# The MLP's operands at another place modulo 512 bytes, a third buffer for the block sums, and four sums in three operations

## The chip, the cores and the metric

The kernel runs on one core of a Trainium2 chip. The metric is the device time of one execution in microseconds (us); of the kernel before, three runs were timed, and the median counts. One more execution was recorded by the hardware profiler; all rows of a trace in this document come from such a recording. Engines are named as in the profile: PE is the matrix engine (PEld its weight loads), DVE the vector engine, ACT the scalar engine, POOL the GpSimd engine, SP the engine that issues most DMAs.

## The reference, cut to what matters

A two-layer encoder on 256 tokens of width 2048, in float32. Each layer has an attention block (neighbourhood attention in layer 0, grouped-query attention in layer 1, both beside four cross-attention heads into 256 memory tokens), an output projection, and a dense MLP of inner width 8192 with a squared ReLU:

```python
h = h + jnp.concatenate([mix, cross], axis=-1) @ w_o[i]
n = rms_norm(h, mlp_norm[i])
h = h + jnp.square(jax.nn.relu(n @ w_up[i])) @ w_down[i]
```

The change touches only what runs in and around the MLP.

## The kernel before, in words

**Precision.** Every float32 product is made of three matmuls in a reduced float32 format: each operand is split into a high and a low half (ACT copies the high half, L302; DVE subtracts it, L303), and high x high, high x low and low x high are added in PSUM. So each weight that comes in by DMA passes ACT and DVE once before PE reads it.

**Two shapes of matmul.** Each matmul has a stationary operand of 128x128, which a weight load (LDWEIGHTS) brings into PE, and a moving operand that streams through. In the first shape the weights stand still and 256 columns of activations move: the MLP's up-projection (L736 to L738, `ps_u<-hT,uh`: hT moves, uh and ul stand still) and the q, k and memory-key projections (L222 to L224, `ps_s`). In the second the activations stand still and 512 columns of weights move: the MLP's down-projection (L852 to L854, `p<-th,a_s`: th moves, a_s stands still), the value and output projections and the last eighth of the down-projection (L210 to L214, `ps_m`).

**The MLP.** The inner width is cut in 8 parts of 8 blocks of 128. `up_grains` computes one block with 48 matmuls (two grains of 24). `squared` applies ReLU and square on ACT, and for each pair of blocks forms four sums of their quarter blocks (L802, tile `c`) and splits seven of the eight quarters into `a_s`. The down-projection of the first seven parts uses a scheme with seven products in place of eight for each pair of blocks (p1 to p7): `down_grains` takes three blocks of weights as they are (tile `b`, split into bh and bl; 9 matmuls, products p3, p1 and p2) and four block sums (tile `t`, split into th and tl; 12 matmuls, products p5, p7, p6 and p4). Of the four sums one is the loaded fourth block plus another, added in the DMA itself (L832, issued on POOL), and three are formed on DVE (L831, L840, L841). At the end of each half part `taken` adds the seven PSUM banks into `h` or into the collectors z (DVE L875, L886, ACT), and `folded` combines the collectors at the very end. The eighth part is done with plain products (`plain_grains`).

**A step.** Outside the first part, the program alternates: 48 up matmuls of one block, then 12 with th and tl, then 9 with bh and bl. There are 56 such steps in a layer, 112 in all. They read, as the built program's allocation has it, at these addresses modulo 512 bytes: hT at 160, uh and ul at 480 and 224 (two buffers), and th, tl, bh, bl and a_s all at 128. (In the attention of layer 0, nT moves at 128 and hi and lo stand at 192 and 448.)

**Order and buffers.** A list of grains with fixed look-ahead (`SOON`) decides when loads, sums and splits are recorded; a scheduler then places the recorded instructions on their engines by its own timeline. Each engine runs its list in order. The tiles of the MLP lie in two pools: `mlp` (z, c, a_s or a_p, bh, bl, th, tl) and `side` (raw weights raw_U, b, t, and the splits uh, ul). The tag `T` in `side` holds t, the scaled rows h_s ahead of the MLP, and half of the plain weights (raw_T); it has two buffers of 8 KB per partition. Loads of t, b and raw_U share the queue of SP, which issues in order and holds there until a buffer is free.

**Names for offsets.** `half_of_side(raw, hf, place)` puts a split at `place` bytes into its buffer. MOVING_AT = 160 puts uh at 128 or 384 modulo 512 where it is the moving operand (plain products, and the first chunks of layer 1's projection); STILL_AT = 64 puts the ring's hi and lo at 192 or 448 where they stand still.

Of the kernel before, what the change touches and what calls it, by code (L numbers as in the profile page):

```python
# [17 lines left out]
P = 128  # L18
# [21 lines left out]
GUARD = 3  # L40

MOVING_AT = 160

STILL_AT = 64
MASKED = -1e30
# [29 lines left out]
def encoder_kernel(ctx: ExitStack, tc: tile.TileContext, t: dict, out: bass.AP):  # L75
# [4 lines left out]
    def opened(name, side="left", space=None, bufs=1):  # L80
        kw = {"space": space} if space else {}
        manager = tc.tile_pool(name=name, bufs=bufs, side=side, reuse_waits="tile", **kw)
        pools[name] = manager, manager.__enter__()
        return pools[name][1]
# [557 lines left out]
    def o_done(layer, nb):  # L642
        which = 2 * layer

        def guard():

            box["near"] = mean_square(which, GUARD, "near")
            box["scale"] = keep.tile([P, NT], F32, tag="scale", name="scale")
            nc.gpsimd.tensor_tensor(box["scale"], box["near"], mhalf[:, :NT], op=ALU.pow)
            box["hT"] = wide(f"hT{layer}")  # L650

        def begun():

            y = at.side.tile([P, NT, 512], F32, tag="T", bufs=2, name="h_s")
            for i in range(NT):
                nc.scalar.activation(y[:, i, :], h[:, i, D - 512 :], AF.Copy, scale=box["scale"][:, i : i + 1])
            box["begun"] = y

        def scaled(b):
            y = at.side.tile([P, NT, 512], F32, tag="T", bufs=2, name="h_s")  # L660
            for i in range(NT):
                nc.scalar.activation(y[:, i, :], h[:, i, b * 512 : (b + 1) * 512], AF.Copy,
                                     scale=box["scale"][:, i : i + 1])
            transposed(box["hT"], lambda i, k: y[:, i, k % 4 * P : (k % 4 + 1) * P],
                       list(range(b * 4, b * 4 + 4)), (G_M0, G_M1)[layer])

        def inv():

            v = mean_square(which, 4, "full")
            box["inv"] = keep.tile([P, NT], F32, tag="inv", name="inv")  # L670
            nc.vector.reciprocal(v, v)
            nc.vector.tensor_tensor(box["inv"], v, box["near"], op=ALU.mult)
            box["ninv"] = keep.tile([P, NT], F32, tag="ninv", name="ninv")
            nc.vector.tensor_scalar(box["ninv"], box["inv"], -1.0, None, op0=ALU.mult)

        def f(w):
            if nb == 0:
                closed("work")
                at.side = opened("side", side="right")
            def add():  # L680
                for i in range(NT):
                    hs = h[:, i, nb * 512 : (nb + 1) * 512]
                    nc.vector.tensor_tensor(hs, w.ps[i], hs, op=ALU.add)

            def squares():
                for i in range(NT):
                    sum_squares(which, i, nb)

            if nb < 3:
                add()  # L690
                squares()
            if nb == GUARD - 1:
                later(1, guard)
                for b in range(GUARD):
                    later(2 + 2 * b, scaled, b)
                later(7, begun)
            if nb == 3:
                y = box["begun"]
                for i in range(NT):
                    nc.vector.scalar_tensor_tensor(y[:, i, :], w.ps[i], box["scale"][:, i : i + 1], y[:, i, :],  # L700
                                                   op0=ALU.mult, op1=ALU.add)
                box["ready"] = transposed(box["hT"], lambda i, k: y[:, i, k % 4 * P : (k % 4 + 1) * P],
                                          list(range(12, KT)), (G_M0, G_M1)[layer])
                later(4, past, add)
                later(6, past, squares)
                later(8, past, inv)
        return f
# [36 lines left out]
        return tiles  # L744

    def loaded(src, tag):
        raw = at.side.tile([P, CH], F32, tag=tag, bufs=2, name=f"raw_{tag}")
        nc.sync.dma_start(raw, src)
        return raw

    def up_grains(layer, part, m):
        own = {}

        def load():
            own["raw"] = loaded(t[f"w_up{layer}"][part * PK + m], "U")

        def prep(hf):
            own[hf] = half_of_side(own["raw"], hf)

        def run(hf):  # L760
            if hf == 0:
                if part == 0:
                    own["ps"] = at.acc.tile([P, 512], F32, tag="acc", name="ps_u")[:, :SEQ]
                else:
                    if part == 1 and m == 0:
                        closed("ps_att", "ps_acc")
                        at.sums = opened("ps_sums", space=bass.MemoryType.PSUM)
                        box["ps"] = {}
                    own["ps"] = at.sums.tile([P, 512], F32, tag="up", name="ps_u")[:, :SEQ]
                    if part == 1 and m == 0:  # L770
                        box["first"] = {n: at.sums.tile([P, 512], F32, tag=n, name=n) for n in BANKS}
            u_products(own["ps"], hf * (KT // 2), KT // 2, *own.pop(hf))

        def after():
            if part == 0 and m == 0:
                closed("cat", "ring")
                at.mlp = opened("mlp")
                box["z"] = [at.mlp.tile([P, 4, 512], F32, tag=f"z{q}", name=f"z{q}") for q in range(2)]
                box["z_set"] = set()
            squared(layer, part, m, own["ps"])  # L780

        return [Grain(lambda: run(0), None, load, None, lambda: prep(0), SOON),
                Grain(lambda: run(1), after, None, None, lambda: prep(1), SOON)]

    def squared(layer, part, m, ps):

        e = m % 2
        if e == 0:
            box["c"] = at.mlp.tile([P, 8, P], F32, tag="c", bufs=2, name="c")
        c = box["c"]  # L790
        two = c[:, 2 * e : 2 * e + 2, :].rearrange("p a b -> p (a b)")
        nc.scalar.activation(two, ps, AF.Relu)
        nc.scalar.activation(two, two, AF.Square)
        if e == 0:
            return
        if part == PARTS - 1:
            a = at.mlp.tile([P, 2, 4, P], F32R, tag="a", bufs=6, name="a_p")
            split(a[:, 0], a[:, 1], c[:, :4])
        else:
            for d, x, y, op in ((4, 2, 0, ALU.subtract), (5, 1, 0, ALU.add), (6, 5, 2, ALU.subtract),  # L800
                                (7, 3, 6, ALU.subtract)):
                nc.vector.tensor_tensor(c[:, d, :], c[:, x, :], c[:, y, :], op=op)  # L802
            a = at.mlp.tile([P, 2, 7, P], F32R, tag="a", bufs=6, name="a_s")
            split(a[:, 0], a[:, 1], c[:, 1:])
        box["a", part, m // 2] = a
        if part == PARTS - 1 and m == PK - 1 and layer == 1:
            later(2, load_gf)

    def down_grains(layer, part, n, begins, ends):
# [4 lines left out]
        def load():  # L814
            src = t[f"w_pair{layer}"][(part * 2 + q) * STEPS + j]
            own["b"] = at.side.tile([P, 3 * 512], F32, tag="b", bufs=2, name="b")
            nc.sync.dma_start(own["b"], src[:, : 3 * 512])
            own["t"] = at.side.tile([P, 4, 512], F32, tag="T", bufs=2, name="t")
            nc.sync.dma_start(own["t"][:, 0, :], src[:, 3 * 512 :])

        def behind(fn):
# [71 lines left out]
    def folded(q):  # L893

        z1, z5, z6, z7 = (box["z"][q][:, n, :] for n in range(4))
        inv, ninv = box["inv"], box["ninv"]
        add_scaled(columns_of(1, q, 0), z1, inv[:, 1:2])
        nc.vector.tensor_tensor(z6, z6, z1, op=ALU.subtract)
        nc.vector.tensor_tensor(z7, z6, z7, op=ALU.subtract)
        nc.vector.tensor_tensor(z6, z6, z5, op=ALU.add)  # L900
        add_scaled(columns_of(1, q, 1), z6, inv[:, 1:2])
        add_scaled(columns_of(0, q, 0), z7, inv[:, 0:1])
        nc.vector.tensor_tensor(z7, z7, z5, op=ALU.add)
        add_scaled(columns_of(0, q, 1), z7, ninv[:, 0:1])

    def plain_grains(layer, nb):
# [8 lines left out]

        def prep(c, hf):
            if c == 0:
                own[c, hf] = half_of_side(own[0], hf, MOVING_AT)
            else:
                own[c, hf] = tuple(at.mlp.tile([P, HALF], F32R, tag="bt"[hf] + x, name=f"{x}_p") for x in "hl")  # L920
                split(*own[c, hf], own[1][:, hf * HALF : (hf + 1) * HALF])
# [351 lines left out]
```

## Time and profile before

| what | value |
|---|---|
| median of 3 runs | 2046.73 us (2046.35 to 2048.07) |
| the profiled execution | 2049.4 us, span 2047.6 us |
| PE busy | 2025.4 us, 99% of the span, 13044 matmuls |
| DVE busy | 1665.1 us, 81% |
| ACT busy | 1241.3 us, 61% |
| chain that ended last | PE 94%, DVE 3%, DMA 1% |

The span runs from the first to the last instruction of the core. A matmul's own duration in the trace holds its latency (0.28 us for 256 columns, 0.39 us for 512), and matmuls overlap; how fast they follow each other is read from their starts. In the answers of the timeline a row has start, duration, engine, line, operation, tiles and count. In a list of waits a row has who waited, for whom, the sum in us, the number of times and the longest. The groups of instructions have busy time and mean duration in ns, then the idle time of the engine ahead of them and who ended it.

### The profile page before, as it was taken

What the parts mean: (1) busy time and instruction counts of PE and PEld (TensorE: products, weight loads), DVE (VectorE), ACT (ScalarE), POOL (GpSimd) and SP (SyncE); (2) the same over time, 40 slices, a digit from 0 to 9 for tenths busy, and PEclk for the clock granted to TensorE, in tenths of its full rate; (3) what the DMA queues carried; (4) which work ended last, traced back from release to release, by engine and by line L of the source; (5) the groups of instructions that cost most, each with busy time, mean ns of one, the idle gap of its engine ahead of it and who ended that gap; (6) DMA issues with size and microseconds to landing.
All of it is one profiled execution on the core that took longest, in us unless ns stands there. A gap on an engine that the chain in (4) does not pass through costs nothing.

```text
span 2047.6 us, 32742 instructions
## 1 busy us (share of the span) xinstructions
PE 2025.4 (99%) x13044; PEld 1831.0 (89%) x13044; DVE 1665.1 (81%) x2049; ACT 1241.3 (61%) x1628; POOL 126.4 (6%) x156
## 2 busy tenths in 40 slices
PE   8999999999999999999999999999999999999998
PEld 7899999889999998999988888889999999999986
DVE  6767677558989889989997667657988999999896
ACT  6655455456666665666656557556666666666654
POOL 0000000000000000010000001000000000000000
PEclk9999999999999999999999999999999999999999
DMA  7756666727777777777765554537777787777773
GB/s 276 281 197 204 217 209 218 287 75 243 229 228 231 214 230 229 226 235 226 235 209 214 176 173 144 199 114 236 233 224 222 227 241 224 240 218 231 227 219 136
DMA packets 101306, 440.16 MB, mean 215 GB/s; under 512 B 11424, under 2 KB 19232, under 8 KB 68000
## 3 DMA queue, kind: packets, MB, share of 16 engines
q1 hardware_dynamic: 82800, 402.40, 58.3%
q0 software_dynamic: 17776, 34.61, 9.0%
q8 instruction: 102, 1.67, 0.3%
q10 hardware_dynamic: 576, 1.05, 0.1%
q14 instruction: 52, 0.43, 0.1%
HBM read 401.32 MB, written 7.34 MB: 200 GB/s over the span
## 4 chain that ended last, share of the span: by engine, by line
PE 94%; DVE 3%; DMA 1%; issue 1%; ACT 1%; SPq 0%; POOLq 0%; POOL 0%; DVEq 0%; ACTq 0%
PE ps_u L738 11%; PE ps_u L736 11%; PE ps_u L737 10%; PE p L853 8%; PE p L852 8%; PE p L854 8%; PE ps_m L210 8%; PE ps_m L213 8%; PE ps_m L214 8%; PE ps_s L222 3%; PE ps_s L224 3%; PE ps_s L223 3%; DVE ul L303 1%; DMA t<-in_w_pair 1%; DVE tl L303 1%
## 5 line engine op out<-in xcount | busy, mean ns | idle before, releaser
L738 PE MATMUL ps_u<-hT,ul 128*128 128x256 f32 x2048 | 568.1, 278 | 2.3 <-DVE ul L303 2.1
L736 PE MATMUL ps_u<-hT,uh 128*128 128x256 f32 x2048 | 568.0, 277 | 0.1
L737 PE MATMUL ps_u<-hT,uh 128*128 128x256 f32 x2048 | 567.3, 277 | 0.0
L302 ACT ACTIVATE uh<-raw_U 128x1024 fp32r<-128x1024 f32 x278 | 294.1, 1060 | 286.2 <-PE ps_u L737 260.9
L738 PEld LDWEIGHTS ps_u<-hT,ul 128*128 128x128 f32 x2048 | 385.4, 188 | 5.3 <-DVE ul L303 4.4
L736 PEld LDWEIGHTS ps_u<-hT,uh 128*128 128x128 f32 x2048 | 384.9, 188 | 5.6 <-ACT uh L302 0.5
L737 PEld LDWEIGHTS ps_u<-hT,uh 128*128 128x128 f32 x2048 | 384.4, 188 | 4.5
L303 DVE TENSOR_TENSOR lo<-raw,hi 128x1024 fp32r<-128x1024 f32 (+1 forms) x224 | 266.3, 1194 | 148.0 <-ACT hi L302 146.4
L303 DVE TENSOR_TENSOR ul<-raw_U,uh 128x1024 fp32r<-128x1024 f32 x278 | 337.1, 1218 | 38.5 <-ACT uh L302 38.4
L302 ACT ACTIVATE hi<-raw 128x1024 fp32r<-128x1024 f32 (+1 forms) x224 | 231.6, 1039 | 203.5 <-PE ps_m L214 112.6
L302 ACT ACTIVATE th<-t 128x2048 fp32r<-128x2048 f32 x112 | 215.2, 1921 | 129.7 <-PE p L854 111.7
L303 DVE TENSOR_TENSOR tl<-t,th 128x2048 fp32r<-128x2048 f32 x112 | 255.9, 2285 | 16.6 <-ACT th L302 16.3
L303 DVE TENSOR_TENSOR bl<-b,bh 128x1536 fp32r<-128x1536 f32 x112 | 196.0, 1750 | 0.3 <-ACT bh L302 0.3
L853 PE MATMUL p<-tl,a_s 128*128 128x512 f32 x448 | 177.6, 396 | 1.2 <-DVE tl L303 1.1
L854 PE MATMUL p<-th,a_s 128*128 128x512 f32 x448 | 174.5, 389 | 0.0
L302 ACT ACTIVATE bh<-b 128x1536 fp32r<-128x1536 f32 x112 | 166.1, 1483 | 6.9 <-PE p L854 1.3
L832 POOL DMA_DIRECT2D t<-b x112 | 96.3, 860 | 1165.1 <-DVE t L831 676.0
L852 PE MATMUL p<-th,a_s 128*128 128x512 f32 x448 | 166.1, 395 | 0.0
L831 DVE TENSOR_TENSOR t<-t,b 128x512 f32<-128x512 f32 x112 | 77.2, 690 | 75.8 <-DMA t<-in_w_pair 59.7
L854 PE MATMUL p<-bh,a_s 128*128 128x512 f32 x336 | 131.1, 390 | 0.0
L853 PE MATMUL p<-bl,a_s 128*128 128x512 f32 x336 | 131.1, 390 | 0.0
L224 PE MATMUL ps_s<-nT,lo 128*128 128x256 f32 x448 | 125.4, 280 | 0.0
(237 smaller groups left out, 3820.7 us busy)
## 6 DMA issues: line engine op xcount, KB each, us to landing
raw_U<-in_w_up SPq DMA_DIRECT2D x128, 1024.0 KB, 6.6
b<-in_w_pair SPq DMA_DIRECT2D x112, 768.0 KB, 4.5
raw<-in_w_o SPq DMA_DIRECT2D x32, 1024.0 KB, 5.0
t<-in_w_pair SPq DMA_DIRECT2D x112, 256.0 KB, 3.6
t<-b POOLq DMA_DIRECT2D x112, 256.0 KB, 6.8
raw<-in_w_b SPq DMA_DIRECT2D x21, 1024.0 KB, 5.0
raw<-in_w_av SPq DMA_DIRECT2D x12, 1024.0 KB, 5.0
raw<-in_w_aq SPq DMA_DIRECT2D x12, 1024.0 KB, 5.0
```

Source lines behind the costliest of these rows:

```text
L210: first = nc.tensor.matmul(w.ps[i], ah, hi[:, s], start=st, stop=False)
L213: nc.tensor.matmul(w.ps[i], ah, lo[:, s], start=False, stop=False)
L214: nc.tensor.matmul(w.ps[i], al, hi[:, s], start=False, stop=sp)
L224: nc.tensor.matmul(ps, lo[:, s], acts[:, k, :SEQ], start=False, stop=k == KT - 1)
L302: first = nc.scalar.activation(dst_hi, src, AF.Copy)
L303: return first, nc.vector.tensor_tensor(dst_lo, src, dst_hi.bitcast(F32), op=ALU.subtract)
L736: nc.tensor.matmul(ps, hi[:, s], acts[:, k, :SEQ], start=k == 0, stop=False)
L737: nc.tensor.matmul(ps, hi[:, s], acts[:, k, SEQ:], start=False, stop=False)
L738: nc.tensor.matmul(ps, lo[:, s], acts[:, k, :SEQ], start=False, stop=k == KT - 1)
L852: nc.tensor.matmul(ps, a[:, 0, ai, :], hi[:, s], start=begins, stop=False)
L853: nc.tensor.matmul(ps, a[:, 0, ai, :], lo[:, s], start=False, stop=False)
L854: nc.tensor.matmul(ps, a[:, 1, ai, :], hi[:, s], start=False, stop=ends)
```

## The change

Three things, and what they need:

- A tile of 192 bytes named `gap` is put at the head of the pool `mlp`. All tiles of this pool move by 192 bytes more than the rest: z, c, a_s, a_p, th, tl, bh, bl, h_p and l_p then lie at 320 modulo 512 bytes. hT, uh and ul stay at 160, 480 and 224. In the plain products the splits of raw_U go to offset 96 in place of 160, which puts them at 64 or 320.
- The tag `T` gets three buffers. The 8 KB for it come from the scratch space of the DMAs that POOL issues (`dynamic_dma_scratch_size`), which is 8192 bytes in place of 16384; everything in the lower part of the memory moves down by 8192 bytes, or 0 modulo 512.
- Of the four sums of `c`, the second and third become one DVE operation of 256 elements (c1 is added to c0 and to c4). For that c4 is formed with the opposite sign, product p5 has the opposite sign, and `folded` subtracts z5 where it added it.

```diff
--- before.py
+++ after.py
@@ -40,6 +40,10 @@
 GUARD = 3
 
 MOVING_AT = 160
+
+PLAIN_AT = 96
+
+MLP_AT = 192
 
 STILL_AT = 64
 MASKED = -1e30
@@ -651,13 +655,13 @@
 
         def begun():
 
-            y = at.side.tile([P, NT, 512], F32, tag="T", bufs=2, name="h_s")
+            y = at.side.tile([P, NT, 512], F32, tag="T", bufs=3, name="h_s")
             for i in range(NT):
                 nc.scalar.activation(y[:, i, :], h[:, i, D - 512 :], AF.Copy, scale=box["scale"][:, i : i + 1])
             box["begun"] = y
 
         def scaled(b):
-            y = at.side.tile([P, NT, 512], F32, tag="T", bufs=2, name="h_s")
+            y = at.side.tile([P, NT, 512], F32, tag="T", bufs=3, name="h_s")
             for i in range(NT):
                 nc.scalar.activation(y[:, i, :], h[:, i, b * 512 : (b + 1) * 512], AF.Copy,
                                      scale=box["scale"][:, i : i + 1])
@@ -744,7 +748,7 @@
         return tiles
 
     def loaded(src, tag):
-        raw = at.side.tile([P, CH], F32, tag=tag, bufs=2, name=f"raw_{tag}")
+        raw = at.side.tile([P, CH], F32, tag=tag, bufs=3 if tag == "T" else 2, name=f"raw_{tag}")
         nc.sync.dma_start(raw, src)
         return raw
 
@@ -775,6 +779,7 @@
             if part == 0 and m == 0:
                 closed("cat", "ring")
                 at.mlp = opened("mlp")
+                at.mlp.tile([P, MLP_AT // 4], F32, tag="gap", name="gap")
                 box["z"] = [at.mlp.tile([P, 4, 512], F32, tag=f"z{q}", name=f"z{q}") for q in range(2)]
                 box["z_set"] = set()
             squared(layer, part, m, own["ps"])
@@ -797,9 +802,9 @@
             a = at.mlp.tile([P, 2, 4, P], F32R, tag="a", bufs=6, name="a_p")
             split(a[:, 0], a[:, 1], c[:, :4])
         else:
-            for d, x, y, op in ((4, 2, 0, ALU.subtract), (5, 1, 0, ALU.add), (6, 5, 2, ALU.subtract),
-                                (7, 3, 6, ALU.subtract)):
-                nc.vector.tensor_tensor(c[:, d, :], c[:, x, :], c[:, y, :], op=op)
+            nc.vector.tensor_tensor(c[:, 4, :], c[:, 0, :], c[:, 2, :], op=ALU.subtract)
+            nc.vector.tensor_tensor(c[:, 5:7, :], c[:, 1:2, :].to_broadcast([P, 2, P]), c[:, 0:5:4, :], op=ALU.add)
+            nc.vector.tensor_tensor(c[:, 7, :], c[:, 3, :], c[:, 6, :], op=ALU.subtract)
             a = at.mlp.tile([P, 2, 7, P], F32R, tag="a", bufs=6, name="a_s")
             split(a[:, 0], a[:, 1], c[:, 1:])
         box["a", part, m // 2] = a
@@ -815,7 +820,7 @@
             src = t[f"w_pair{layer}"][(part * 2 + q) * STEPS + j]
             own["b"] = at.side.tile([P, 3 * 512], F32, tag="b", bufs=2, name="b")
             nc.sync.dma_start(own["b"], src[:, : 3 * 512])
-            own["t"] = at.side.tile([P, 4, 512], F32, tag="T", bufs=2, name="t")
+            own["t"] = at.side.tile([P, 4, 512], F32, tag="T", bufs=3, name="t")
             nc.sync.dma_start(own["t"][:, 0, :], src[:, 3 * 512 :])
 
         def behind(fn):
@@ -897,10 +902,10 @@
         add_scaled(columns_of(1, q, 0), z1, inv[:, 1:2])
         nc.vector.tensor_tensor(z6, z6, z1, op=ALU.subtract)
         nc.vector.tensor_tensor(z7, z6, z7, op=ALU.subtract)
-        nc.vector.tensor_tensor(z6, z6, z5, op=ALU.add)
+        nc.vector.tensor_tensor(z6, z6, z5, op=ALU.subtract)
         add_scaled(columns_of(1, q, 1), z6, inv[:, 1:2])
         add_scaled(columns_of(0, q, 0), z7, inv[:, 0:1])
-        nc.vector.tensor_tensor(z7, z7, z5, op=ALU.add)
+        nc.vector.tensor_tensor(z7, z7, z5, op=ALU.subtract)
         add_scaled(columns_of(0, q, 1), z7, ninv[:, 0:1])
 
     def plain_grains(layer, nb):
@@ -915,7 +920,7 @@
 
         def prep(c, hf):
             if c == 0:
-                own[c, hf] = half_of_side(own[0], hf, MOVING_AT)
+                own[c, hf] = half_of_side(own[0], hf, PLAIN_AT)
             else:
                 own[c, hf] = tuple(at.mlp.tile([P, HALF], F32R, tag="bt"[hf] + x, name=f"{x}_p") for x in "hl")
                 split(*own[c, hf], own[1][:, hf * HALF : (hf + 1) * HALF])
@@ -1260,7 +1265,7 @@
         arrays[f"w_pair{i}"] = pair_chunks(a["w_down"][i][:split_at])
         arrays[f"w_plain{i}"] = plain_chunks(a["w_down"][i][split_at:])
 
-    nc = _bacc.Bacc("TRN2", target_bir_lowering=False, num_devices=1)
+    nc = _bacc.Bacc("TRN2", target_bir_lowering=False, num_devices=1, dynamic_dma_scratch_size=8192)
     t = {
         n: nc.dram_tensor(f"in_{n}", v.shape, mybir.dt.from_np(v.dtype), kind="ExternalInput").ap()
         for n, v in arrays.items()
```

## The prediction

> **What bounds the kernel now.** First the page: busy times, the granted clock and the chain of waits.
>
> ```profile
> span 2047.6 us, 32742 instructions
> ...
> PE 2025.4 (99%) x13044; PEld 1831.0 (89%) x13044; DVE 1665.1 (81%) x2049; ACT 1241.3 (61%) x1628; POOL 126.4 (6%) x156
> ...
> PEclk9999999999999999999999999999999999999999
> ...
> PE 94%; DVE 3%; DMA 1%; issue 1%; ACT 1%; SPq 0%; POOLq 0%; POOL 0%; DVEq 0%; ACTq 0%
> ```
>
> PE is busy throughout at full clock, and 94% of the chain is PE. So there are two ways to gain: the few stalls, and the pace at which matmuls follow each other. Busy shares do not show the pace, so next I read starts in the timeline of PE, over one step of layer 0's MLP: the first up matmul, the sixth, the first with th, the first with bh, and the first of the next step.
>
> ```profile
> 983.44 0.28 PE L736 MATMUL ps_u<-hT,uh 128*128 128x256 f32 x1
> ...
> 984.04 0.28 PE L738 MATMUL ps_u<-hT,ul 128*128 128x256 f32 x1
> ...
> 988.92 0.40 PE L852 MATMUL p<-th,a_s 128*128 128x512 f32 x1
> ...
> 991.70 0.39 PE L852 MATMUL p<-bh,a_s 128*128 128x512 f32 x1
> ...
> 993.74 0.28 PE L736 MATMUL ps_u<-hT,uh 128*128 128x256 f32 x1
> ```
>
> The first five up matmuls take 0.60 us, 0.120 each. The other 43 take 4.88, 0.1135 each. The twelve with th take 2.78, 0.2317 each, and the nine with bh 2.04, 0.2267 each. Nothing waits here, so some matmuls run slower than others of the same shape. What is the clean pace? Two stretches of the same instruction in layer 0's attention, with 84 matmuls between the first two starts and 117 between the last two; and twelve matmuls of the plain products at the end.
>
> ```profile
> 170.06 0.28 PE L224 MATMUL ps_s<-nT,lo 128*128 128x256 f32 x1
> ...
> 179.58 0.28 PE L365 MATMUL sc_ps<-kT,qT 128*128 128x256 f32 x1
> ...
> 225.93 0.28 PE L224 MATMUL ps_s<-nT,lo 128*128 128x256 f32 x1
> ...
> 239.71 0.28 PE L365 MATMUL sc_ps<-kT,qT 128*128 128x256 f32 x1
> ...
> 2033.20 0.39 PE L210 MATMUL ps_m<-uh,a_p 128*128 128x512 f32 x1
> ...
> 2035.92 0.39 PE L210 MATMUL ps_m<-h_p,a_p 128*128 128x512 f32 x1
> ```
>
> 9.52/84 = 0.1133 and 2.72/12 = 0.2267 are clean; 13.78/117 = 0.1178 is not. The two stretches have the same tile names, shapes and residues modulo 512, and yet one keeps 4.5 ns more per matmul for 14 us. So there is a slow mode of 256 columns that can persist, and what came before decides which mode is entered: 170.06 follows scores, 225.93 follows a mix of values and attention products.
>
> A step at clean pace is 48 x 0.1133 + 21 x 0.2267 = 10.20 us; the one above took 10.30. The 0.10 lie where the shape changes: 0.033 in the first five up matmuls, 0.06 in the twelve with th. After that PE is clean until the next change. Over 49 steps of layer 1:
>
> ```profile
> 1438.60 0.28 PE L736 MATMUL ps_u<-hT,uh 128*128 128x256 f32 x1
> ...
> 1943.96 0.28 PE L736 MATMUL ps_u<-hT,uh 128*128 128x256 f32 x1
> ```
>
> 505.36/49 = 10.313, so 0.113 above clean. Times 112 steps that is **12.7 us**, all that a better address can win in the MLP. The mean is above 0.10 because some steps ride the slow mode, like the 46 up matmuls from 703.06 (0.1178 each):
>
> ```profile
> 703.06 0.28 PE L738 MATMUL ps_u<-hT,ul 128*128 128x256 f32 x1
> ...
> 708.48 0.39 PE L852 MATMUL p<-th,a_s 128*128 128x512 f32 x1
> ...
> 711.22 0.39 PE L852 MATMUL p<-bh,a_s 128*128 128x512 f32 x1
> ```
>
> Last the waits: PE's in the whole run, DVE's, and the place of PE's longest wait in the MLP.
>
> ```profile
> PE ps_u L738 <- DVE ul L303: 2.1, 4, 0.8
> PE p L853 <- DVE tl L303: 1.1, 2, 0.6
> ...
> DVE t L831 <- DMA t<-in_w_pair: 59.7, 67, 2.6
> ...
> 764.54 0.69 DVE L831 TENSOR_TENSOR t<-t,b 128x512 f32<-128x512 f32 x1 [1.93 <-DMA t<-in_w_pair]
> ...
> 775.04 0.69 DVE L831 TENSOR_TENSOR t<-t,b 128x512 f32<-128x512 f32 x1 [0.35 <-DMA t<-in_w_pair]
> ...
> 781.04 2.28 DVE L303 TENSOR_TENSOR tl<-t,th 128x2048 fp32r<-128x2048 f32 x1
> ...
> 783.38 0.50 PE L853 MATMUL p<-tl,a_s 128*128 128x512 f32 x1 [0.64 <-DVE tl L303]
> ```
>
> In most steps DVE has time to spare, and its 59.7 us of waiting for t cost nothing. At the end of a part it also empties the PSUM banks; then 2.28 us of such waiting end, some steps later, in PE waiting for tl.
>
> **The addresses.** Nothing is added to the path: the gap is no instruction. Within the second shape both operands move together, so th to bh, and th or bh to the plain products, keep their relation, and PLAIN_AT keeps it for uh. What changes is each step's two jumps: up to th, where the moving address went from 160 to 128 and now goes from 160 to 320 (64 modulo 256), and bh to up, the way back. The weights' jumps are 480 or 224 to 128 before, to 320 now. No row shows these jumps, so bounds come from rows of others. The best: no cost, as between uh and h_p above, where the jump keeps the shape; that is -12.7 us. The worst: all up matmuls ride the slow mode, 48 x 0.0045 = 0.21 us, and the th that follow cost 0.02 (2.74 against 2.72 at 708.48); 0.234 - 0.113 = 0.121 more per step, **+13.5** us. Between them stands the other direct jump from 256 to 512 columns, from the memory keys to the memory values, where the moving operand stays at 128 and the weights go from 192 or 448 to 128:
>
> ```profile
> 79.49 0.40 PE L210 MATMUL ps_m<-hi,memT 128*128 128x512 f32 x1
> ...
> 80.87 0.39 PE L210 MATMUL ps_m<-hi,memT 128*128 128x512 f32 x1
> ```
>
> Six matmuls in 1.38 against 1.36: 0.02 where th costs 0.06. So the cost does depend on the place, and by this much. I take 0.02 for the way to th, and 0.04 for the way back, about as now (0.033): 0.06 per step in place of 0.113, times 112 is **-6 us**.
>
> The Trainium skill speaks against this term: "SBUF — State Buffer", section "Who interferes with whom", has PE wait on nobody, and "TensorE: Matmul & The Clock Gate", Part 2, gives PE two independent read ports, so that loading the next weights takes nothing from the running matmul. By that the sum has 0 here. The trace differs: 0.1178 and 0.1133 for the same work.
>
> **The third buffer.** At the start of the MLP, SP issues three loads of t ahead in place of two, then all else in the old order. Its queue (before, then after):
>
> ```order
> L159 DMA raw<-in_w_o 128x2048 x6
> L819 DMA t<-in_w_pair 128x512 x2
> L748 DMA raw_U<-in_w_up 128x2048 x6
> L817 DMA b<-in_w_pair 128x1536
> L748 DMA raw_U<-in_w_up 128x2048
> ```
>
> ```order
> L163 DMA raw<-in_w_o 128x2048 x6
> L824 DMA t<-in_w_pair 128x512 x3
> L752 DMA raw_U<-in_w_up 128x2048 x6
> L822 DMA b<-in_w_pair 128x1536
> L752 DMA raw_U<-in_w_up 128x2048
> ```
>
> So t lands a step (10.3 us) sooner, and the scheduler moved the sums with it. On DVE at an end of a part in layer 0 (L831, L840 and L841 before are L836, L845 and L846 after; L303 is L307):
>
> ```order
> L886 TENSOR_TENSOR z_4687<-p_7355,z_4687 128x512
> L875 SCALAR_TENSOR_TENSOR h<-p_7359,inv,h 128x512
> L802 TENSOR_TENSOR c<-c 128x128
> L841 TENSOR_TENSOR t<-t,b 128x512
> L303 TENSOR_TENSOR tl<-t,th 128x2048
> L303 TENSOR_TENSOR bl<-b,bh 128x1536
> L303 TENSOR_TENSOR a_s<-c,a_s 128x896
> L303 TENSOR_TENSOR ul<-raw_U,uh 128x1024 x2
> ```
>
> ```order
> L891 TENSOR_TENSOR z_4688<-p_7342,z_4688 128x512
> L880 SCALAR_TENSOR_TENSOR h<-p_7346,inv,h 128x512
> L806 TENSOR_TENSOR c<-c 128x256
> L836 TENSOR_TENSOR t<-t,b 128x512
> L307 TENSOR_TENSOR tl<-t,th 128x2048
> L307 TENSOR_TENSOR bl<-b,bh 128x1536
> L807 TENSOR_TENSOR c<-c 128x128
> L845 TENSOR_TENSOR t<-t,b 128x512
> L307 TENSOR_TENSOR ul<-raw_U,uh 128x1024 x2
> ```
>
> The three sums ahead of a tl are now those of the step behind it; tl's own were formed a step sooner. Late next would be ul, behind one sum more, but without the a_s ahead of it. What can be won is PE's wait for tl (1.1 us), the slow restart behind each, and smaller ones; 0 to -3. The 2.28 us that DVE no longer waits exceed the longest chain's 0.64, so I take half of the range, **-1.5 us**. The waits for ul (2.1) fall at the start of each MLP, where the change moves little: 0.
>
> **The sums of c, and the rest.** The groups by line:
>
> ```profile
> L840 DVE TENSOR_TENSOR t<-t,b 128x512 f32<-128x512 f32 x112 | 76.8, 685 | 1.0
> ...
> L802 DVE TENSOR_TENSOR c<-c 128x128 f32<-128x128 f32 x224 | 58.9, 284 | 1.0
> ...
> L832 POOL DMA_DIRECT2D t<-b x112 | 96.3, 860 | 1165.1 <-DVE t L831 676.0
> ```
>
> 256 elements cost, on the line between 284 ns (128) and 685 (512), 418 ns: 2 x 284 - 418 = 150 ns less for each of 56 pairs, 8.4 us of DVE, of which only what lies at the ends of parts reaches PE; it is in the -1.5. The signs in `folded` cost nothing. The smaller scratch: POOL issues one accumulating DMA per step, 0.86 us in 10.3, so its space is rarely shared; 0, at worst some 1 us where layer 1's memory tiles come back together.
>
> Sum: 2049.4 - 6 - 1.5 = 2041.9 for a profiled execution. That one lay 2.7 above the median, so the forecast is **2039.2**.
>
> **Rivals.** Clean jumps: both new jumps cost next to nothing, as between uh and h_p; -12.7 - 1.5 gives 2032.5. For it: clean stretches exist in both shapes; against: every direct jump of shape that I read costs something.
>
> The address does nothing: the jumps cost as now, only the stall term is left, 2045.2. For it: what moves is a whole multiple of 64 bytes for both operands of the second shape; against: 0.02 and 0.06 for two jumps of the same kind. The skill's rule would give this time too.
>
> Slower, by one mechanism: the jump from bh back to up now enters the slow mode, as 703.06 and 225.93 did, and 48 matmuls are too few to leave it (117 were). It decides at the first up matmuls of a step; if all steps enter it, +13.5 - 1.5 gives 2058.7, and it outweighs the stall term from one step in nine on. For it: jumps that I cannot tell apart by their residues entered it; against: in the steady step PE left it after five.
>
> **How the numbers follow.** A measurement of this kernel tells about 0.2% (4.1 us) from no change. Half-won jumps (2036 to 2042): 0.42; clean jumps 0.15; nothing 0.24; slow mode, in part or in all steps, 0.19. Faster: 0.42 + 0.15 + a little of the third, 0.58; within: 0.24; slower: 0.18. The likeliest has 2035 to 2043; the range reaches to the clean case and into the slow one, 2031 to 2053.
>
> **What would show it.** In the profile after: starts of a steady step, 10.26 us by the forecast, 10.20 in the clean case, 10.30 if nothing changed, 10.43 in the slow mode; twelve th in 2.74 and not 2.78; five or more up matmuls at 0.118 or not; PE's wait for tl near 0, and DVE's wait for t far below 59.7 us; c in three groups, the middle one near 418 ns. Wrong would be a step above 10.30, or a wait of PE for ul or tl that is new.

## The result: slower by 1.9%, and the profile after

The changed kernel takes 2084.93 us (median of 4 runs, 2083.92 to 2088.21) against 2047.10 for the kernel before, timed beside it: a ratio of 1.0186, 95% interval 1.0174 to 1.0198. The forecast was 2039.2 with a range to 2053. The profiled execution took 2084.58 us.

The page of the kernel after:

```profile
span 2082.8 us, 32690 instructions
...
PE 2041.8 (98%) x13044; PEld 1824.0 (88%) x13044; DVE 1660.7 (80%) x1993; ACT 1237.6 (59%) x1628; POOL 125.4 (6%) x156
...
PE 66%; DVE 15%; DMA 12%; issue 5%; ACT 1%; SPq 0%; DVEq 0%; POOLq 0%; POOL 0%; ACTq 0%
DMA b<-in_w_pair 11%; PE ps_m L214 8%; PE ps_m L217 8%; PE ps_m L218 8%; PE ps_u L742 6%; PE ps_u L740 6%; PE ps_u L741 6%; DVE bl L307 5%; PE p L858 4%; PE p L859 4%; DVE tl L307 4%; PE p L857 3%; PE ps_s L226 3%; PE ps_s L228 3%; PE ps_s L227 3%
```

PE is still 98% busy, but its share of the chain of waits fell from 94% to 66%. The load of b, the three plain blocks, has 11% of it, where all DMA had 1%.

The waits of PE, then of DVE, in the whole run after (who waited, for whom, sum in us, times, longest):

```profile
PE p L858 <- DVE tl L307: 17.7, 28, 1.7
```

```profile
DVE t L836 <- DMA b<-in_w_pair: 130.1, 93, 3.7
```

PE's wait for tl was to vanish and grew from 1.1 us to 17.7. DVE's wait for t (59.7 us) did vanish, as forecast, and a wait for b of 130.1 us took its place, in 93 steps of 112.

How much of the loss is in the MLP shows in the windows over the MLPs of the two layers: first of the kernel before, then of the kernel after (length, PE busy and matmuls, and so on).

```profile
496.00:1064.00 568.00, 567.09 (x3790) 517.31 (x3789) 519.47 (x555) 364.20 (x367) 45.59 (x53) 1.00 0.76 227
1428.00:1995.00 567.00, 566.51 (x3789) 517.75 (x3788) 520.43 (x557) 364.66 (x367) 45.42 (x53) 1.00 0.76 228
```

```profile
496.00:1064.00 568.00, 558.98 (x3688) 499.98 (x3687) 504.46 (x520) 353.80 (x357) 45.63 (x53) 1.00 0.73 222
1428.00:1995.00 567.00, 555.45 (x3664) 495.98 (x3663) 498.13 (x516) 350.86 (x355) 44.56 (x52) 1.00 0.73 223
```

In the same time PE starts 102 and 125 matmuls fewer. At 0.15 us each (568.00/3790) that is 34 of the 35.2 us by which the span grew. PE's busy time falls by 19.2 us only: a matmul's own time holds its latency, so a stall shorter than that does not show as idle. The count of what was done is the better measure here.

And where nothing stalls, the steps are as forecast. Starts of one step of the kernel after in layer 0: first up matmul, first with th, first with bh, the next up, the next th.

```profile
731.71 0.28 PE L740 MATMUL ps_u<-hT,uh 128*128 128x256 f32 x1
...
737.16 0.39 PE L857 MATMUL p<-th,a_s 128*128 128x512 f32 x1
...
739.92 0.84 PE L857 MATMUL p<-bh,a_s 128*128 128x512 f32 x3
...
741.97 0.28 PE L740 MATMUL ps_u<-hT,uh 128*128 128x256 f32 x1
...
747.42 0.39 PE L857 MATMUL p<-th,a_s 128*128 128x512 f32 x1
```

5.45 + 2.76 + 2.05 = 10.26 us, against 10.30 before. So one part of the change works, and another one costs some 45 us.

### The profile page after: what moved, and what is told of

It is laid out like the page before. It is cut to its first block, busy times and chain, and to the rows that moved or that the text cites. A ratio compares the mean times of both kernels' runs of the same rounds, so it can differ in the third digit from the quotient of the medians.

```text
span 2082.8 us, 32690 instructions
## 1 busy us (share of the span) xinstructions
PE 2041.8 (98%) x13044; PEld 1824.0 (88%) x13044; DVE 1660.7 (80%) x1993; ACT 1237.6 (59%) x1628; POOL 125.4 (6%) x156
## 4 chain that ended last, share of the span: by engine, by line
PE 66%; DVE 15%; DMA 12%; issue 5%; ACT 1%; SPq 0%; DVEq 0%; POOLq 0%; POOL 0%; ACTq 0%
DMA b<-in_w_pair 11%; PE ps_m L214 8%; PE ps_m L217 8%; PE ps_m L218 8%; PE ps_u L742 6%; PE ps_u L740 6%; PE ps_u L741 6%; DVE bl L307 5%; PE p L858 4%; PE p L859 4%; DVE tl L307 4%; PE p L857 3%; PE ps_s L226 3%; PE ps_s L228 3%; PE ps_s L227 3%
## 5 line engine op out<-in xcount | busy, mean ns | idle before, releaser
L307 DVE TENSOR_TENSOR ul<-raw_U,uh 128x1024 fp32r<-128x1024 f32 x278 | 331.3, 1218 | 38.1 <-ACT uh L306 37.9
L858 PE MATMUL p<-tl,a_s 128*128 128x512 f32 x448 | 182.4, 407 | 18.8 <-DVE tl L307 17.7
L836 DVE TENSOR_TENSOR t<-t,b 128x512 f32<-128x512 f32 x112 | 77.3, 691 | 130.1 <-DMA b<-in_w_pair 130.1
L859 PE MATMUL p<-th,a_s 128*128 128x512 f32 x448 | 175.5, 392 | 0.0
L857 PE MATMUL p<-th,a_s 128*128 128x512 f32 x448 | 156.7, 393 | 0.0
L858 PEld LDWEIGHTS p<-tl,a_s 128*128 128x128 f32 x448 | 84.0, 188 | 56.1 <-DVE tl L307 40.2
L859 PE MATMUL p<-bh,a_s 128*128 128x512 f32 x336 | 132.0, 393 | 0.0
```

The lines of the kernel that those rows point to most:

```text
L307: return first, nc.vector.tensor_tensor(dst_lo, src, dst_hi.bitcast(F32), op=ALU.subtract)
L857: nc.tensor.matmul(ps, a[:, 0, ai, :], hi[:, s], start=begins, stop=False)
L858: nc.tensor.matmul(ps, a[:, 0, ai, :], lo[:, s], start=False, stop=False)
L859: nc.tensor.matmul(ps, a[:, 1, ai, :], hi[:, s], start=False, stop=ends)
```

## Where the time goes: a loop through the two rooms of b

DVE in the kernel after, over one step, from its timeline:

```profile
590.25 1.75 DVE L307 TENSOR_TENSOR bl<-b,bh 128x1536 fp32r<-128x1536 f32 x1
...
596.28 0.69 DVE L836 TENSOR_TENSOR t<-t,b 128x512 f32<-128x512 f32 x1 [1.02 <-DMA b<-in_w_pair]
597.01 0.69 DVE L845 TENSOR_TENSOR t<-t,b 128x512 f32<-128x512 f32 x1
597.62 2.29 DVE L307 TENSOR_TENSOR tl<-t,th 128x2048 fp32r<-128x2048 f32 x1
599.82 0.69 DVE L846 TENSOR_TENSOR t<-t,b 128x512 f32<-128x512 f32 x1
600.42 1.08 DVE L307 TENSOR_TENSOR a_s<-c,a_s 128x896 fp32r<-128x896 f32 x1
601.43 1.75 DVE L307 TENSOR_TENSOR bl<-b,bh 128x1536 fp32r<-128x1536 f32 x1
```

The chain of waits over the same stretch (start, length, what):

```profile
590.33 1.68 DVE bl L307
...
592.03 4.16 DMA b<-in_w_pair
...
596.28 0.70 DVE t L836
...
600.42 1.08 DVE a_s L307
601.51 1.68 DVE bl L307
...
603.21 4.26 DMA b<-in_w_pair
```

Number the steps by k. A step's b has two rooms (the two buffers of its tag), so the load of b(k+2) goes into the room of b(k), and SP can issue it when bl(k) has read that. In most steps of the kernel before, DVE ran bl(k), the three sums of step k+1, then tl(k): those sums need b(k+1), which had a whole step to arrive. With a third room for t, the first sum of step k+2 stands between bl(k) and tl(k) in 104 of 112 steps (counted in the order of the built program). It needs b(k+2), which bl(k) has only just made room for. DVE runs its list in order, so tl(k) stands behind that wait, and bl(k+1), which makes room for the next load, stands behind tl(k). That closes a loop with a round per step: bl, load, sum, tl, bl. From 590.25 to 601.43 one round takes 11.18 us, where a step of PE takes 10.26.

One round alone shows no loss, since rounds are unequal: in e3, the run below that keeps all but the order, they go mostly from 9.2 to 11.3 us and cost PE nothing. The mean does show it. The bl of steps 1 and 54 of layer 0 (counted from 0), in the change and then in e3:

```profile
490.49 1.75 DVE L307 TENSOR_TENSOR bl<-b,bh 128x1536 fp32r<-128x1536 f32 x1
...
1056.56 1.75 DVE L307 TENSOR_TENSOR bl<-b,bh 128x1536 fp32r<-128x1536 f32 x1
```

```profile
488.20 1.75 DVE L307 TENSOR_TENSOR bl<-b,bh 128x1536 fp32r<-128x1536 f32 x1
...
1033.32 1.75 DVE L307 TENSOR_TENSOR bl<-b,bh 128x1536 fp32r<-128x1536 f32 x1
```

566.07/53 is 10.68 us a round against 545.12/53 = 10.29; in layer 1 it is 10.76 against 10.29. In both layers together the 106 rounds lose 46.3 us, nearly all of the 46.5 by which the span of the change (2082.8) is longer than that of e3 (2036.3).

PE then waits for tl, here in the second of the twelve matmuls with th and tl:

```profile
576.94 0.40 PE L857 MATMUL p<-th,a_s 128*128 128x512 f32 x1
578.80 0.50 PE L858 MATMUL p<-tl,a_s 128*128 128x512 f32 x1 [1.47 <-DVE tl L307]
```

The load itself is no slower; the two rows are of the kernel before and after:

```profile
b<-in_w_pair SPq DMA_DIRECT2D x112, 768.0 KB, 4.5
```

```profile
b<-in_w_pair SPq DMA_DIRECT2D x112, 768.0 KB, 4.4
```

## The experiments

Theory: the order of DVE closes the loop, and the two rooms of b carry it. Rivals: (1) the new addresses slow PE; (2) the smaller scratch or the fused sums do it; (3) a third load of t in flight slows the loads; (4) sums that stand early are bad in themselves. All ratios are against the kernel before, timed on the same chip beside each group of runs (medians 2046.38, 2045.94 and 2046.56).

**e1: T back at two rooms.**

```diff
-            y = at.side.tile([P, NT, 512], F32, tag="T", bufs=3, name="h_s")
+            y = at.side.tile([P, NT, 512], F32, tag="T", bufs=2, name="h_s")
...
-        raw = at.side.tile([P, CH], F32, tag=tag, bufs=3 if tag == "T" else 2, name=f"raw_{tag}")
+        raw = at.side.tile([P, CH], F32, tag=tag, bufs=2, name=f"raw_{tag}")
...
-            own["t"] = at.side.tile([P, 4, 512], F32, tag="T", bufs=3, name="t")
+            own["t"] = at.side.tile([P, 4, 512], F32, tag="T", bufs=2, name="t")
```

> The change with the tag T back at two rooms; addresses, fused sums and the smaller scratch stay. Theory (a loop through the two rooms of b): with the third room the sums of the next step stand ahead of this step's tl on DVE and wait for a load of b that bl alone can release; with two rooms of T they stand behind bl again, so PE's wait for tl falls from 17.7 us to under 2, DVE's wait for b from 130 us to near 0, and the address gain shows (10.26 us per undisturbed step in the trace after, against 10.31 before): 2041 us, 2037 to 2044. Rival 1 (the new addresses slow PE): it stays at 2078 or more. Rival 2 (the smaller scratch or the fused sums do it): it stays at 2078 or more too.

Measured: 2042.06 us, ratio 0.9981 (0.9971 to 0.9990). In its lists PE's wait for tl is 1.5 us and no wait for b is left. Rivals 1 and 2 fall: addresses, fused sums and scratch are all in this kernel.

**e2: the third room alone, on the kernel before.**

```diff
-            own["t"] = at.side.tile([P, 4, 512], F32, tag="T", bufs=2, name="t")
+            own["t"] = at.side.tile([P, 4, 512], F32, tag="T", bufs=3, name="t")
...
-    nc = _bacc.Bacc("TRN2", target_bir_lowering=False, num_devices=1)
+    nc = _bacc.Bacc("TRN2", target_bir_lowering=False, num_devices=1, dynamic_dma_scratch_size=8192)
```

> The kernel before with the third room for T and the smaller scratch that pays for it; old addresses, four separate sums. Theory (loop): as slow as the change less its address gain, 2088 us (2084 to 2095), PE's wait for tl 15 us or more, DVE's wait for b over 100 us. Rival 1 (addresses) and the fused sums as the cause: 2046 to 2048, as before.

Measured: 2081.57 us, ratio 1.0175 (1.0157 to 1.0192), a little below the range given. The group of its first sum (busy us, mean ns, then idle ahead of it and who ended that):

```profile
L831 DVE TENSOR_TENSOR t<-t,b 128x512 f32<-128x512 f32 x112 | 77.5, 692 | 121.1 <-DMA b<-in_w_pair 121.1
```

So the third room alone gives nearly all of the loss. PE's wait for tl was 11.4 us and not 15, and one of 7.5 us for ul was there too. That it is not slower than the change by the 6 us of the addresses fits the loop, though no run shows it by itself: while a round takes longer than PE's work, a faster PE only waits longer.

**e3: the third room, but the sums tied behind bl of the step before.** (Tied: the scheduler may place them only behind that instruction.)

```diff
-            return (lambda: past(fn, box["splits"][-4])) if part == 0 and n < 2 else fn
+            if part == 0 and n < 2:
+                return lambda: past(fn, box["splits"][-4])
+            return (lambda: past(fn, box["last_bl"])) if fn is pre else fn
...
-            split(*own["first"], own["b"])
+            box["last_bl"] = split(*own["first"], own["b"])
```

> The change with all three rooms, but the sums of a step are tied in order behind the split bl of the step before, where they stood in the kernel before. Theory (the order closes the loop, not the room): as with two rooms, 2041 us (2036 to 2044), PE's wait for tl under 2 us, DVE's wait for b near 0. Rival 3 (the third load of t in flight, or the smaller scratch, slows the loads themselves): stays above 2065.

Measured: 2038.36 us (2038.10 to 2039.33), ratio 0.9961 (0.9947 to 0.9976): faster than both kernels, and 46.6 us faster than the change with the same rooms, loads, addresses and scratch (46.0 by the two ratios). The lists of SP and POOL are the same; on DVE the sums stand elsewhere, and with them some of the small operations beside them (c, a_s); ACT and PE run some neighbours in another order. (The added lines move L836 to L846 and L857 to L859 by two: the first sum is L838.) The chain of its page, and the group of the first sum (with the idle time ahead of it last):

```profile
PE 96%; DVE 1%; DMA 1%; ACT 1%; issue 1%; SPq 0%; POOLq 0%; POOL 0%; ACTq 0%
```

```profile
L838 DVE TENSOR_TENSOR t<-t,b 128x512 f32<-128x512 f32 x112 | 76.8, 685 | 0.0
```

The first sum waits for nothing, neither t nor b, and no wait for tl is left in PE's list. In the window 496 to 1064 PE starts 3810 matmuls, 122 more than the change and 20 more than the kernel before:

```profile
496.00:1064.00 568.00, 568.00 (x3810) 519.39 (x3809) 525.78 (x541) 366.01 (x369) 45.73 (x53) 1.00 0.76 231
```

Rival 3 falls.

**e4: a third room for b too, nothing tied.**

```diff
-            own["b"] = at.side.tile([P, 3 * 512], F32, tag="b", bufs=2, name="b")
+            own["b"] = at.side.tile([P, 3 * 512], F32, tag="b", bufs=3, name="b")
...
-    nc = _bacc.Bacc("TRN2", target_bir_lowering=False, num_devices=1, dynamic_dma_scratch_size=8192)
+    nc = _bacc.Bacc("TRN2", target_bir_lowering=False, num_devices=1, dynamic_dma_scratch_size=2048)
```

> The change with a third room for b as well (scratch 2048 bytes, to pay for its 6 KB); nothing tied. Theory (loop): the load of b no longer waits for bl of the step but one before, so the loop is open whatever the order: 2041 us (2036 to 2046), DVE's wait for b under 20 us. Rival 3 (the loads themselves are slower with more of them ahead and less scratch): stays above 2065, and more so with the still smaller scratch.

Measured: 2042.31 us, ratio 0.9979 (0.9969 to 0.9988). As the theory has it, but this run alone proves little: with three rooms the scheduler chose another order, bl(k), all three sums of step k+2, tl(k). There the sums stand a full step earlier than in the kernel before, and the loss is gone. DVE now waits for t again, 62.1 us, and PE for tl 2.5 and for ul 3.4.

**e5 and e6: the sums early by force, with two rooms of b and with three.** The look-ahead of the sums is 7 grains in place of 5, and what leads to tl(k) (the second and third sum, th, tl) is tied behind the first sum of a later step; e6 has the rooms of e4 besides.

```diff
-            nc.vector.tensor_tensor(s[:, 1, :], s[:, 0, :], block(0), op=ALU.add)
+            own["sum"] = box["first_sum"] = nc.vector.tensor_tensor(s[:, 1, :], s[:, 0, :], block(0), op=ALU.add)
...
         def prep_second():
-            s = own["t"]
+            s, front = own["t"], box["first_sum"]
+            if front is not own["sum"] and (part or n > 1):
+                with tc.issue_after(front.ins):
+                    prep_tl(s)
+            else:
+                prep_tl(s)
+
+        def prep_tl(s):
...
-    SOON = (8, 5, 4)
+    SOON = (8, 7, 4)
```

> The change with two rooms of b and three of T, and an order tied so that one sum more lies between a load of b and tl: on DVE bl of a step, then at once the first sum that needs the next load into the room that this bl gives free, then the second sum of another step, then tl. Theory (loop of bl, load of b, sum, tl, per step): the loop grows by one sum, 0.69 us, over that of the change; where the change lost 46.5 us against e3 (0.42 us in each of 112 steps), this one loses up to 0.69 x 112 = 77 us more: 2160 us, at least 2110. Rival (what hurts is only that the sums stand early, whatever they wait for, or a busy DMA): about as the change, 2075 to 2095.

> The same tie as the run before it, but with a third room for b (and 2048 bytes of scratch): the first sum after bl now needs a load whose room was given free a step earlier. Theory (loop): nothing waits for bl, so 2041 us (2037 to 2046), DVE's wait for b under 20 us, PE's wait for tl under 4 us. Rival (sums that stand early are bad in themselves): 2070 or more, as without the third room.

e5 measured 2091.26 us, ratio 1.0222 (1.0202 to 1.0243): my number was at least 2110, and the rival's range holds it. The tie gave the intended order in 40 steps only, 1 to 20 of each layer (in the order of the built program); DVE waits for b in 54 steps and not 93, and for 72.3 us. As a test of the loop's length it failed. The bl of steps 1 and 21 of layer 0:

```profile
490.53 1.75 DVE L307 TENSOR_TENSOR bl<-b,bh 128x1536 fp32r<-128x1536 f32 x1
...
709.00 1.76 DVE L307 TENSOR_TENSOR bl<-b,bh 128x1536 fp32r<-128x1536 f32 x1
```

218.47/20 is 10.92 us a round. The same rounds take 10.84 in the change and 10.30 in e3; in layer 1 it is 10.93, 10.94 and 10.30. So the rounds in the forced order are longer than a step, but not by 0.69 us longer than those of the change. The 40 of them lose 25 us on e3, half of the 50 by which the span is longer (2086.4 against 2036.3). Where the other half comes from was not settled.

e6 measured 2039.66 us, ratio 0.9966 (0.9953 to 0.9979). Here the first sum of step k+2 stands between bl(k) and tl(k), ahead of the other sums, in 104 steps, earlier than in the change, and nothing waits for b, since b(k+2) now goes into the room of b(k-1). That rules out rival 4: early sums cost nothing when their load does not hang on the bl just before.

**e7 and e8: the two other parts alone, on the kernel before.** e7 has the gap and PLAIN_AT and nothing else; e8 the third room, the smaller scratch and the tie of e3.

> The kernel before with the gap of 192 bytes and the splits at 96 and nothing else. By the prediction's first term 6 us less than before; by the starts of steps in the trace after that no wait disturbed (10.26 us, against a mean of 10.31 before) 5.6 us less: 2041 us, 2039 to 2044. Rival (PE is indifferent to addresses): 2046.4, as before.

> The kernel before with the third room of T, the smaller scratch, and the sums tied behind bl; old addresses, four separate sums. If the gain of e3 over e1 (3.7 us) is the room's own, it is there without the addresses too: 2043 us (2041 to 2045), with PE's wait for tl near 0. If it comes from the fused sums or needs the new addresses: 2046 to 2047.

e7: 2040.15 us, ratio 0.9968 (0.9956 to 0.9981), 6.5 us by the ratio, 5.8 by the medians. e8: 2045.11, ratio 0.9992 (0.9983 to 1.0001): 0.8 us by the medians, 1.6 by the ratio, not told from none, though PE's wait for tl is gone. The gain of 3.7 us that I read between e1 and e3 is therefore not all the room's: e1's ten runs spread from 2039.55 to 2043.84.

**e9: e3 with four sums again.**

```diff
-            nc.vector.tensor_tensor(c[:, 5:7, :], c[:, 1:2, :].to_broadcast([P, 2, P]), c[:, 0:5:4, :], op=ALU.add)
+            nc.vector.tensor_tensor(c[:, 5, :], c[:, 1, :], c[:, 0, :], op=ALU.add)
+            nc.vector.tensor_tensor(c[:, 6, :], c[:, 1, :], c[:, 4, :], op=ALU.add)
```

> e3 with the sums of c as four operations of 128 columns again. By the prediction the fused operation takes 8 us from DVE and nothing from the path: 2038.4, as e3 (2037 to 2040). Rival (DVE is tight at the ends of parts, so 150 ns less there reaches PE): 2040 to 2043, with new waits of PE for tl or ul.

Measured: 2038.97 us, ratio 0.9963 (0.9950 to 0.9977); not told from e3. The fused sums are off the path.

**e10 to e12: e3 at other places modulo 512.** Only the two constants change (MLP_AT and PLAIN_AT: 32 and 192, 96 and 0, 160 and 64); every engine's order is that of e3.

> e3 with the MLP's tiles at 160 modulo 512 in place of 320, the place of hT (gap 32, splits of the plain products at 192); the order of every engine is the same. If the cost of a jump of shape goes by how far the moving address jumps: no jump is left, as between the memory keys and values (0.02 us for six matmuls), so a step costs 10.22 to 10.25 in place of 10.26, 2034 to 2037 us. If it goes by the single place: anything between the clean 2031 and the slow mode's 2060; 2046 or more would show that 320 was a good choice and not just another one.

> e3 with the MLP's tiles at 224 modulo 512 (gap 96, splits of the plain products at 0), the place of one of the two buffers of uh and ul; same order. By the distance of the moving addresses (64 from hT, 160 in e3, 32 in the kernel before): between the two, 2038 to 2044. By the single place: open, 2031 to 2060.

> e3 with the MLP's tiles at 288 modulo 512 (gap 160, splits of the plain products at 64), 32 below e3; same order. If the place counts modulo 64: like the old place's odd half, 2041 to 2044. If 320 is good by a wide margin: 2038.4, as e3.

Measured: 2059.80 us (ratio 1.0065, 1.0051 to 1.0078), 2055.27 (1.0043, 1.0029 to 1.0056) and 2055.96 (1.0046, 1.0032 to 1.0060). All three are slower than the kernel before. Neither the distance from hT's place nor the place modulo 64 gave the right number. Starts over a step of e3, then of e12:

```profile
982.84 0.39 PE L859 MATMUL p<-th,a_s 128*128 128x512 f32 x1
...
985.60 0.84 PE L859 MATMUL p<-bh,a_s 128*128 128x512 f32 x3
...
987.65 0.28 PE L740 MATMUL ps_u<-hT,uh 128*128 128x256 f32 x1
...
993.10 0.39 PE L859 MATMUL p<-th,a_s 128*128 128x512 f32 x1
```

```profile
1022.73 0.39 PE L859 MATMUL p<-th,a_s 128*128 128x512 f32 x1
...
1025.45 0.84 PE L859 MATMUL p<-bh,a_s 128*128 128x512 f32 x3
...
1027.49 0.28 PE L740 MATMUL ps_u<-hT,uh 128*128 128x256 f32 x1
...
1033.14 0.61 PE L859 MATMUL p<-th,a_s 128*128 128x512 f32 x2
```

At 288 (e12) the matmuls with th and bh are clean, 2.72 and 2.04, where e3 has 2.76 and 2.05. But the 48 up matmuls take 5.65 and not 5.45: 0.1177 each, the slow mode, for all 48. 10.41 - 10.26 is 0.15 us, times 112 some 17 us; measured are 17.6. The group of one of the three up lines says it for all steps, in e3 and in e12 (mean 277 and 281 ns):

```profile
L742 PE MATMUL ps_u<-hT,ul 128*128 128x256 f32 x2048 | 566.9, 277 | 1.7 <-DVE ul L307 1.5
```

```profile
L742 PE MATMUL ps_u<-hT,ul 128*128 128x256 f32 x2048 | 574.9, 281 | 1.7 <-DVE ul L307 1.5
```

## Why the prediction was wrong

**The addresses, -6 us: right in size, by luck in its parts.** Alone they gave 5.8 to 6.5 us (e7), and a step without a stall takes the 10.26 us of the forecast. But the division of the 0.06 us was off, and that the parts add up to it was luck: th costs 0.04 in place of the 0.02 I took, bh 0.01 where I had nothing, the way back to up 0.01 and not 0.04. The rule of the Trainium skill ("SBUF — State Buffer", section "Who interferes with whom") by which PE never waits on anyone, and by which the prediction would have put 0 here, does not cover this: e3 and e12 run the same instructions in the same order, 17.6 us apart.

**The third buffer, -1.5 us: this step failed.** In the change it cost about 46 us (2084.93 against 2038.36 of e3), through the order that came with it. I read rightly that sums move a step ahead and that DVE's wait for t goes. I then priced the term by the wait removed, and took "late next would be ul" without asking what the moved sum itself reads. It reads t and b. t had a third room; b had not, and in the new place its load can start only at the bl just ahead. "The three sums ahead of a tl are now those of the step behind it" was a misreading of the order shown there. In the kernel before, the sums ahead of a tl were those of the step behind it already. What is new in the list after is the L836 just ahead of tl: by the built program it is the first sum of step 30, and the tl is that of step 28. So the third buffer moved the sum to behind the one bl that its load waits for.

The rows of before would have given a price. On DVE, from its groups of instructions there:

```profile
L303 DVE TENSOR_TENSOR tl<-t,th 128x2048 fp32r<-128x2048 f32 x112 | 255.9, 2285 | 16.6 <-ACT th L302 16.3
L303 DVE TENSOR_TENSOR bl<-b,bh 128x1536 fp32r<-128x1536 f32 x112 | 196.0, 1750 | 0.3 <-ACT bh L302 0.3
L831 DVE TENSOR_TENSOR t<-t,b 128x512 f32<-128x512 f32 x112 | 77.2, 690 | 75.8 <-DMA t<-in_w_pair 59.7 <-issue 11.5 <-DVE ul L303 4.6
...
L303 DVE TENSOR_TENSOR a_s<-c,a_s 128x896 fp32r<-128x896 f32 x56 | 60.7, 1083 | 0.0
```

bl 1.75, the load 4.5 (from issue to landing), the sum ahead of tl and one behind it 2 x 0.69, tl 2.29: 9.92 us. By the built order of the change, 104 such rounds hold 240 sums in place of 208, and 28 of them a_s (1.08) besides: 0.21 and 0.29 us more on average. The mean of 10.42 is longer than the step of 10.26, and over 104 rounds that is 17 us of loss: the right sign and about a third of the size. The sums of c and the additions into h and z, 60 operations in these rounds, come to another 0.3 us a round by an estimate from their mean durations; that makes 10.7, where 10.68 and 10.76 were measured. The Trainium skill states what makes the loop bind ("TensorE: Matmul & The Clock Gate", the table of figures ahead of Part 1: VectorE's queue is strictly first in, first out), and the trace agrees: tl at 597.62 stood behind L836 and its wait of 1.02 us.

**The room's own worth, where the order is kept:** e8 against before is -0.8 by the medians, e9 against e7 -1.2, e3 against e1 -3.7. The -1.5 of the forecast was a fair size for an order that the change did not have.

**The fused sums and the scratch, 0: right.** The middle operation takes 421 ns against 418 estimated. The 8.4 us of DVE were too much: the busy time of all sums of c falls only from 58.9 to 55.5 us. In the kernel before these operations overlap one another (224 of 284 ns would be 63.6).

```profile
L806 DVE TENSOR_TENSOR c<-c 128x256 f32<-128x256 f32 x56 | 23.6, 421 | 1.1
...
L807 DVE TENSOR_TENSOR c<-c 128x128 f32<-128x128 f32 x56 | 16.1, 287 | 0.8
L805 DVE TENSOR_TENSOR c<-c 128x128 f32<-128x128 f32 x56 | 15.8, 282 | 0.0
```

**The rivals.** The slower one (the slow mode all through the up matmuls, 2058.7) had the sign of the result but not its cause: at 320 the jump back costs 0.01 us. Its mechanism and its price are real at three other places: 2055 to 2060 in e10 to e12. What I had written as the sign of being wrong, a wait of PE for tl that is new, is what came; but no rival of mine led there. All that I allowed on the slower side was about PE, none of it about a load.

## What to carry to other kernels

- When a change gives one operand another room and the order moves, list every operand of the moved instruction, and for each the room that its load goes into and the instruction that gives this room free. If that one stands a step or less ahead on the same in-order engine, add up the round (release, load, work, next release) and compare it with the step.
- A wait that vanishes from an engine with time to spare is worth nothing; what stands in its place can be worth a lot. Here 75.8 us of idle DVE cost next to nothing, and the 130.1 us that replaced them cost 46, because they lay in a loop.
- If the order is the cause, keep the change and tie the order: one tie brought e3 to 2038.4 us, 8 us under the kernel before.

## What the runs showed that was not expected

The place of an operand modulo 512 bytes decides between two paces of the same matmuls, over whole stages. With hT at 160 and the down-projection's operands at 320 (e3), 128 (as before), 224, 288 and 160, the kernel takes 2038.4, 2045.1 (e8, with four sums), 2055.3, 2056.0 and 2059.8 us. In the step of the kernel before that the prediction shows, the up matmuls left the slow mode after five; at 160, 224 and 288 they stay in it for all 48 (5.65 us in a step of each). The places that keep th clean (224 and 288, 2.72 us) put up into the slow mode, and the one that keeps up clean (320) costs th 0.04 us. Whether a place exists that is clean in both (10.20 us a step, 7 us less) and what in the addresses decides, the period of 512 bytes included, was not settled.
